# A hybrid decoder layer on one core: sums of the gate and up weights moved from VectorE to accumulating transfers

## The chip, the core and the metric

The kernel runs on one core of one Trainium2 chip. Four of its engines matter here: TensorE (PE, with its weight loads PEld), VectorE (DVE), ScalarE (ACT) and GpSimd (POOL). SyncE (SP) computes nothing and issues the loads from memory. The metric is the time of one execution on the device in microseconds (us); lower is better.

## The reference

A sequence of 16 meta tokens and 512 tokens of width 1024 goes through a half-step SwiGLU feed-forward block, a token mixer (RG-LRU and a convolution, merged by gates), and a second SwiGLU block. Only the two feed-forward blocks are touched:

```python
def swiglu_ffn(h, w_gu, w_down):
    gate, up = jnp.split(h @ w_gu, 2, axis=-1)
    return (jax.nn.silu(gate) * up) @ w_down

h = h + 0.5 * swiglu_ffn(rmsnorm(h, ffn1_norm[l]), ffn1_w_gu[l], ffn1_w_down[l])
h = h + token_mixer(rmsnorm(h, mix_norm[l]), ...)
h = h + 0.5 * swiglu_ffn(rmsnorm(h, ffn2_norm[l]), ffn2_w_gu[l], ffn2_w_down[l])
```

`w_gu` has 1024 rows and 2 x 2816 columns, all in float32.

## The kernel before

**Products.** A float32 product is made from two float32r parts of each operand: a high part (`hi`, a copy by ScalarE) and a low part (`lo`, value minus high part, by VectorE in the feed-forward blocks), in three passes of TensorE.

**Duo groups.** Gate and up are worked off in groups of 256 columns each. The first three groups of each block are plain products. The other eight of each block, 16 in all, go through `duo`: gate and up, each cut into an upper and a lower half of the 1024 rows, form a 2 x 2 block matrix, the tokens' two halves form the other operand, and the result is made with 7 block products in place of 8 (Winograd's form of Strassen's scheme). Each block product has 24 matmuls and takes one "chunk" of weights, 128 partitions x 1024 float32 (512 KB). The seven chunks of a group are four raw blocks or sums of them. In the first feed-forward block the duo groups stand in runs of 1, 4 and 3, with the down projection behind each run; in the second block all eight follow each other.

**Weights.** The class `Weights` holds the whole list of groups. `load` issues a group's loads on SP into the pool `rawp` (7 tiles); `_split` makes the `hi` and `lo` tiles of one chunk (pool `partp`, 5 tiles of each); `take` hands a chunk to the products and keeps three chunks split ahead. Before a chunk that is a sum, `_sums` has VectorE add or subtract raw tiles: per duo group four such operations of 128 x 1024 (`sum1`, `sum2` twice, `sum4`), into the raw tiles themselves and one tile of the pool `sump`.

**Order.** Each engine works off its own queue strictly in order. The order is set when the program is built, by a scheduler that places instructions as soon as it believes their operands ready; it follows the code's order closely inside a duo group. What a duo group puts on ScalarE besides the `hi` copies are the copies of partial results out of PSUM (`g1`, `u2`, `g2` from `al` and `ga`), two Silus, and the `hi` copies of the results (`ah`). The copy of `al` into `g1` must be done before the group's third product, which adds to the same `al`.

Of the kernel before, what the change touches and what calls it, by code (L numbers as in the profile page):

```python
# [9 lines left out]
F32 = mybir.dt.float32  # L10
F32R = mybir.dt.float32r
AF = mybir.ActivationFunctionType
ALU = mybir.AluOpType

P = 128
# [6 lines left out]
DFF = 2816  # L22
# [4 lines left out]
RG_C = 8.0  # L27
UNIT = 544
NUNITS = 61
NRAW = 7  # L30
SUMS_AHEAD = 1
PLAIN1 = 6
PLAIN2 = 6
AHEAD = 3
# [6 lines left out]
CH = 1024  # L41


class Weights:
# [2 lines left out]

    def __init__(self, nc, raw_pool, part_pool, groups, ahead):  # L50
        self.nc, self.raw_pool, self.part_pool = nc, raw_pool, part_pool
        self.groups = groups
        self.chunks = [(g, c) for g, grp in enumerate(groups) for c in range(len(grp["chunks"]))]
        self.ahead = ahead
        self.pin = None
        self.raw = {}
        self.made = {}
        self.next_group = 0
        self.next_chunk = 0
        self.next_sum = 0  # L60
        self.taken = 0

    @staticmethod
# [11 lines left out]
    def load(self, between=None):  # L75
        g = self.next_group
        pieces = []
        i = 0
        for q, (shape, srcs) in enumerate(self.groups[g]["loads"]):
            view = self.shaped(self.raw_pool.tile([P, CH], F32, tag="wraw", name=f"wraw{g}_{q}"), shape)  # L80
            for at, src in srcs:
                self.nc.sync.dma_start(out=view[at] if at is not None else view, in_=src)
                if between is not None:
                    between(i)
                i += 1
            pieces.append(view)
        self.raw[g] = pieces
        self.next_group += 1

# [1 line left out]
        while self.next_group <= min(g, len(self.groups) - 1):  # L91
            self.load()

    def _sums(self, upto):

        while self.next_sum < min(upto, len(self.chunks)):
            g, c = self.chunks[self.next_sum]
            pre = self.groups[g].get("sums", {}).get(c)
            if pre is not None:
                self._loaded(g)  # L100
                pre(self.raw[g])
            self.next_sum += 1

    def _split(self):
        i = self.next_chunk
        g, c = self.chunks[i]
        self._loaded(g + 1)
        self._sums(i + 1)
        grp = self.groups[g]
        src = grp["chunks"][c](self.raw[g])  # L110
        shape = list(src.shape)
        out = []
        for part in ("hi", "lo"):
            flat = self.part_pool.tile([P, CH], F32R, tag="w" + part, name=f"w{part}{i}")
            out.append(self.shaped(flat, shape))
        hi, lo = out
        ins = self.nc.scalar.activation(hi, src, AF.Copy)  # L117
        if self.pin is not None:
            self.pin(ins)
        eng = self.nc.gpsimd if grp["lo"] == "pool" else self.nc.vector  # L120
        ins = eng.tensor_tensor(lo, src, hi.bitcast(F32), op=ALU.subtract)  # L121
        if self.pin is not None and grp["lo"] != "pool":
            self.pin(ins)
        self.made[i] = (hi, lo)
        self.next_chunk += 1
        if self.pin is None:
            self._sums(i + 1 + SUMS_AHEAD)

    def fill(self):
        while self.next_chunk < min(self.taken + self.ahead, len(self.chunks)):  # L130
            self._split()

    def take(self):
        i = self.taken
        while self.next_chunk < min(i + 1 + self.ahead, len(self.chunks)):
            self._split()
        self.taken += 1
        return self.made.pop(i)


# [1 line left out]
def layer_kernel(ctx, tc, a, out):  # L142
# [1 line left out]
    cpool = ctx.enter_context(tc.tile_pool(name="cpool", bufs=1))  # L144
    upool = ctx.enter_context(tc.tile_pool(name="upool", bufs=NUNITS))
    rawp = ctx.enter_context(tc.tile_pool(name="rawp", bufs=NRAW))
    sump = ctx.enter_context(tc.tile_pool(name="sump", bufs=1))
    partp = ctx.enter_context(tc.tile_pool(name="partp", bufs=5))
    psum = ctx.enter_context(tc.tile_pool(name="psum", bufs=3, space=bass.MemoryType.PSUM))
    psum1 = ctx.enter_context(tc.tile_pool(name="psum1", bufs=2, space=bass.MemoryType.PSUM))  # L150
# [57 lines left out]
    def kview(w, k0, nk, c0, ncol):  # L208
        return w[k0 * P:(k0 + nk) * P, c0:c0 + ncol].rearrange("(k p) m -> p k m", p=P)
# [6 lines left out]
    def duo_group(w, f):  # L216


        hk = KT // 2
        loads = [((P, hk, 2 * P), [(None, kview(w, k0, hk, c0, 2 * P))])  # L220
                 for c0, k0 in ((f * P, 0), (DFF + f * P, 0), (DFF + f * P, hk), (f * P, hk))]
        held = {}

        def sum1(raws):
            g1, u1, u2, g2 = raws
            s1 = Weights.shaped(sump.tile([P, CH], F32, tag="wsum", name=f"wsum{count[0]}"), (P, hk, 2 * P))
            count[0] += 1
            held["s1"] = s1
            nc.vector.tensor_tensor(s1, u1, u2, op=ALU.add)

        def sum2(raws):
            g1, u1, u2, g2 = raws
            nc.vector.tensor_tensor(u1, g1, u1, op=ALU.subtract)
            nc.vector.tensor_tensor(g1, held["s1"], g1, op=ALU.subtract)

        def sum4(raws):
            g1, u1, u2, g2 = raws
            nc.vector.tensor_tensor(g2, g2, g1, op=ALU.subtract)

        chunks = [lambda r: r[0], lambda r: held["s1"], lambda r: r[0], lambda r: r[3], lambda r: r[1],  # L240
                  lambda r: r[3], lambda r: r[2]]
        groups.append(dict(loads=loads, chunks=chunks, lo="dve", sums={1: sum1, 2: sum2, 5: sum4}))

    thirds = [(0, 8), (8, 16), (16, 22)]
    for f0, f1 in thirds:
# [286 lines left out]
    def operands(ops, src, norm, r, th):  # L532

        hk = KT // 2
        b = {}

        def quarter(kh):
            for i in range(hk // 2):
                for t in range(2):
                    b[kh, t, i] = pair("xq", th)  # L540
                for j in range(2):
                    k = kh * hk + 2 * i + j
                    for t in range(2):
                        cut = slice(t * th, (t + 1) * th)
                        nc.vector.scalar_tensor_tensor(b[kh, t, i][:, j, :], src[k][:, cut], norm(k), r[:, cut],
                                                       op0=ALU.mult, op1=ALU.mult)

        def minus(eng, x, y, out=None):

            o = [out[i] if out is not None else pair("xt", th) for i in range(2)]  # L550
            for i in range(2):
                eng.tensor_tensor(o[i], x[i], y[i], op=ALU.subtract)
            return o

        def parts(x):
            out = []
            for i in range(2):
                hi, lo = pair("bh", th, F32R), pair("bl", th, F32R)
                nc.scalar.activation(hi, x[i], AF.Copy)
                nc.vector.tensor_tensor(lo, x[i], hi.bitcast(F32), op=ALU.subtract)  # L560
                out += [(hi[:, j, :], lo[:, j, :]) for j in range(2)]
            return out

        def q(kh, t):
            return [b[kh, t, i] for i in range(2)]
        quarter(0)
        yield
        ops[1] = parts(q(0, 0))
        t1 = minus(nc.vector, q(0, 1), q(0, 0))
        yield  # L570
        ops[5] = parts(t1)
        yield
        quarter(1)
        yield
        t2 = minus(nc.vector, q(1, 1), t1)
        ops[6] = parts(t2)
        yield
        t3 = minus(nc.vector, q(1, 1), q(0, 1), q(0, 1))
        ops[2] = parts(q(1, 0))
        yield  # L580
        t4 = minus(nc.vector, q(1, 0), t2, q(1, 0))
        ops[7] = parts(t3)
        yield
        ops[3] = parts(q(1, 1))
        ops[4] = parts(t4)

    def duo(ops, th, scale=None):

        def times(p, ps, first, last):
            whi, wlo = weights.take()  # L590
            for j in range(2):
                cols = slice(j * P, (j + 1) * P)
                for k in range(KT // 2):
                    xhi, xlo = ops[p][k]
                    for n, (w, xx) in enumerate(((whi, xhi), (whi, xlo), (wlo, xhi))):
                        nc.tensor.matmul(ps[:, j, :th], w[:, k, cols], xx,  # L596
                                         start=(first and k == 0 and n == 0),
                                         stop=(last and k == KT // 2 - 1 and n == 2), skip_group_check=True)
# [17 lines left out]
        times(3, ga, False, True)  # L616
        nc.vector.tensor_tensor(g2, ga[:, :, :th], g2, op=ALU.add)
        nc.scalar.activation(g2, g2, AF.Silu)
        if scale is None:
            nc.vector.tensor_tensor(g2, u2, g2, op=ALU.mult)  # L620
        else:
            nc.vector.scalar_tensor_tensor(g2, u2, scale, g2, op0=ALU.mult, op1=ALU.mult)
        times(4, al, False, True)
        if scale is None:
            nc.vector.tensor_tensor(g1, al[:, :, :th], g1, op=ALU.mult)
        else:
            nc.vector.scalar_tensor_tensor(g1, al[:, :, :th], scale, g1, op0=ALU.mult, op1=ALU.mult)
        return g1, g2

    def split_pairs(pairs, th):  # L630
# [448 lines left out]
```

## Time and profile before

| | |
|---|---|
| median of 3 runs | 1195.04 us (1194.33 to 1195.42) |
| the profiled execution | 1196.02 us, of which the span from first to last instruction is 1194.2 us |
| TensorE busy | 1168.1 us, 98% of the span |
| VectorE busy | 828.7 us, 69% |
| ScalarE busy | 536.6 us, 45% |
| GpSimd busy | 263.4 us, 22%, none of it in the duo groups |
| moved by DMA | 115.24 MB |

The profile is of one execution. Busy time of an engine is the time in which one of its instructions ran; idle time matters only on the engine that sets the end, and there the profile names what ended each wait.

### The profile page before, as it was taken

What the parts mean: (1) busy time and instruction counts of PE and PEld (TensorE: products, weight loads), DVE (VectorE), ACT (ScalarE), POOL (GpSimd) and SP (SyncE); (2) the same over time, 40 slices, a digit from 0 to 9 for tenths busy, and PEclk for the clock granted to TensorE, in tenths of its full rate; (3) what the DMA queues carried; (4) which work ended last, traced back from release to release, by engine and by line L of the source; (5) the groups of instructions that cost most, each with busy time, mean ns of one, the idle gap of its engine ahead of it and who ended that gap; (6) DMA issues with size and microseconds to landing.
All of it is one profiled execution on the core that took longest, in us unless ns stands there. A gap on an engine that the chain in (4) does not pass through costs nothing.

```text
span 1194.2 us, 18531 instructions
## 1 busy us (share of the span) xinstructions
PE 1168.1 (98%) x7723; PEld 1072.6 (90%) x7723; DVE 828.7 (69%) x1051; ACT 536.6 (45%) x703; POOL 263.4 (22%) x144
## 2 busy tenths in 40 slices
PE   7999999999999999999989999999999999999997
PEld 6999999999999999998878887878779999998886
DVE  7987468744866799978986907555697787882223
ACT  5544146522545523356666417433444555572113
POOL 5000000000007455565545843442000000000000
PEclk9999999999999999999989999999999999999999
DMA  8515124422253233332223323333212424253201
GB/s 231 159 33 156 50 72 135 130 89 64 65 151 110 84 95 89 94 101 64 78 88 100 95 88 89 90 96 96 89 54 71 142 72 142 71 177 100 76 1 70
DMA packets 165226, 115.24 MB, mean 96 GB/s; under 512 B 3927, under 2 KB 161015, under 8 KB 165143
## 3 DMA queue, kind: packets, MB, share of 16 engines
q1 hardware_dynamic: 163936, 112.74, 31.5%
q8 instruction: 60, 0.98, 0.3%
q10 hardware_dynamic: 1207, 1.33, 0.3%
q14 instruction: 23, 0.19, 0.0%
HBM read 111.95 MB, written 2.10 MB: 96 GB/s over the span
## 4 chain that ended last, share of the span: by engine, by line
PE 89%; DVE 5%; ACT 3%; DMA 1%; issue 1%; SPq 0%; DVEq 0%; ACTq 0%
PE al L596 15%; PE fin L975 10%; PE down L305 10%; PE ga L596 8%; PE g L305 6%; PE gluv L305 4%; PE glug L305 4%; PE be L596 4%; PE ya L305 4%; PE yb L305 4%; PE wo L305 3%; PE up L305 3%; PE gy L305 3%; PE sgb L305 3%; PE gate L305 3%; PE sga L305 2%
## 5 line engine op out<-in xcount | busy, mean ns | idle before, releaser
L117 ACT ACTIVATE whi<-wraw 128x1024 fp32r<-128x1024 f32 (+2 forms) x244 | 254.5, 1045 | 519.5 <-issue 134.8
L121 DVE TENSOR_TENSOR wlo<-wraw,whi 128x1024 fp32r<-128x1024 f32 (+1 forms) x164 | 198.5, 1212 | 140.6 <-ACT whi L117 136.2
L121 POOL TENSOR_TENSOR wlo<-wraw,whi 128x1024 fp32r<-128x1024 f32 (+1 forms) x80 | 204.8, 2564 | 204.9 <-ACT whi L117 204.8
L713 DVE SCALAR_TENSOR_TENSOR conv<-v,par,conv 128x512 f32<-128x512 f32 x240 | 159.2, 747 | 0.0
L596 PE MATMUL al<-bh,whi 128*128 128x264 f32 (+1 forms) x512 | 144.9, 283 | 0.0
L596 PE MATMUL al<-bl,whi 128*128 128x264 f32 (+1 forms) x512 | 144.9, 283 | 0.0
L596 PE MATMUL al<-bh,wlo 128*128 128x264 f32 (+1 forms) x512 | 144.6, 282 | 0.0
L347 POOL TENSOR_TENSOR sq<-sq,sq 128x528 f32<-128x528 f32 (+1 forms) x18 | 28.1, 1559 | 354.0 <-ACT sq L344 353.9
L596 PEld LDWEIGHTS al<-bh,whi 128*128 128x128 f32 x512 | 96.5, 189 | 0.1
L596 PEld LDWEIGHTS al<-bh,wlo 128*128 128x128 f32 x512 | 96.6, 189 | 0.0
L596 PEld LDWEIGHTS al<-bl,whi 128*128 128x128 f32 x512 | 96.4, 188 | 0.0
L305 PE MATMUL down<-al,whi 128*128 128x264 f32 x352 | 72.3, 286 | 2.1 <-DVE al L636 2.1
L596 PE MATMUL ga<-bh,wlo 128*128 128x264 f32 (+1 forms) x256 | 72.5, 283 | 0.0
L596 PE MATMUL ga<-bl,whi 128*128 128x264 f32 (+1 forms) x256 | 72.4, 283 | 0.0
L596 PE MATMUL ga<-bh,whi 128*128 128x264 f32 (+1 forms) x256 | 72.2, 282 | 0.0
L305 PE MATMUL down<-ah,wlo 128*128 128x264 f32 x352 | 71.5, 284 | 0.0
L305 PE MATMUL down<-ah,whi 128*128 128x264 f32 x352 | 71.4, 284 | 0.0
L305 PEld LDWEIGHTS down<-al,whi 128*128 128x128 f32 x352 | 54.9, 188 | 2.6 <-DVE al L636 2.5
L305 PEld LDWEIGHTS down<-ah,wlo 128*128 128x128 f32 x352 | 54.7, 189 | 0.0
L305 PEld LDWEIGHTS down<-ah,whi 128*128 128x128 f32 x352 | 54.5, 188 | 0.0
L684 DVE SCALAR_TENSOR_TENSOR h<-down,h 128x528 f32<-128x528 f32 x24 | 17.0, 708 | 52.4 <-PE down L305 52.4
L596 PEld LDWEIGHTS ga<-bh,whi 128*128 128x128 f32 x256 | 48.3, 189 | 0.0
(278 smaller groups left out, 2937.1 us busy)
## 6 DMA issues: line engine op xcount, KB each, us to landing
wraw<-in_ffn_w_gu_dram SPq DMA_DIRECT2D x86, 512.0 KB
wraw<-in_w_in_dram SPq DMA_DIRECT2D x48, 512.0 KB
wraw<-in_ffn_w_down_dram SPq DMA_DIRECT2D x38, 512.0 KB
wraw<-in_rnn_w_proj_dram SPq DMA_DIRECT2D x8, 512.0 KB
wraw<-in_conv_w_proj_dram SPq DMA_DIRECT2D x8, 512.0 KB
wraw<-in_w_out_dram SPq DMA_DIRECT2D x8, 512.0 KB
wraw<-in_ffn_w_down_dram SPq DMA_DIRECT2D x8, 384.0 KB
x<-in_x_dram SPq DMA_DIRECT2D x8, 256.0 KB
```

Of the source, the lines that this page charges most:

```text
L117: ins = self.nc.scalar.activation(hi, src, AF.Copy)
L121: ins = eng.tensor_tensor(lo, src, hi.bitcast(F32), op=ALU.subtract)
L305: pin(nc.tensor.matmul(o, w, xx[:, tok] if isinstance(tok, slice) else xx[tok], start=(first and n == 0), stop=(last and n == 2)))
L347: (eng or nc.gpsimd).tensor_tensor(acc, acc, sq, op=ALU.add)
L596: nc.tensor.matmul(ps[:, j, :th], w[:, k, cols], xx, start=(first and k == 0 and n == 0), stop=(last and k == KT // 2 - 1 and n == 2), ski ...
L684: nc.vector.scalar_tensor_tensor(halves(h[m]), ps[:, :, :TH], 0.5, halves(h[m]), op0=ALU.mult, op1=ALU.add)
L713: pin(nc.vector.scalar_tensor_tensor(box[i], v[i][:, k:k + SEQ], pcol("conv_dw_w", k * KT + j + i), box[i], op0=ALU.mult, op1=ALU.add))
L975: nc.tensor.matmul(accs[t][c][:, cols], aa[t // 2][:, t % 2 * P:(t % 2 + 1) * P], w[:, c * SEQ + cols.start:c * SEQ + cols.stop], start=Fa ...
```

## The change

The four sums of each duo group are no longer made by VectorE. A raw tile is loaded, and a transfer issued by GpSimd then reads a second block from memory and adds it onto that tile (`accum_op=ALU.add`). Tile 0 is loaded with a21 (up, upper rows), a22 is added at once (chunk 0); after chunk 0 has been split a11 is added (chunk 2), and after chunk 2 a12 (chunk 5). Tile 1 is loaded with a11 (chunk 1), and after chunk 1 a21 is added (chunk 4). a12 and a22 are also loaded as they are (chunks 3 and 6). So a group has four loads as before and four more transfers of 512 KB. [...] The first product takes chunk 1 and the second chunk 0 (`take(1)`). The raw pool has 8 tiles in place of 7, and the pool `sump` is gone.

```diff
-NRAW = 7
-SUMS_AHEAD = 1
+NRAW = 8
...
             pieces.append(view)
+        for piece, src in self.groups[g].get("adds", {}).get(-1, ()):
+            self.nc.gpsimd.dma_start(out=pieces[piece], in_=src, accum_op=ALU.add)
         self.raw[g] = pieces
...
         self.made[i] = (hi, lo)
         self.next_chunk += 1
-        if self.pin is None:
-            self._sums(i + 1 + SUMS_AHEAD)
+        for piece, src in grp.get("adds", {}).get(c, ()):
+            self.nc.gpsimd.dma_start(out=self.raw[g][piece], in_=src, accum_op=ALU.add)
...
-        loads = [((P, hk, 2 * P), [(None, kview(w, k0, hk, c0, 2 * P))])
-                 for c0, k0 in ((f * P, 0), (DFF + f * P, 0), (DFF + f * P, hk), (f * P, hk))]
-        held = {}
-
-        def sum1(raws):
-            g1, u1, u2, g2 = raws
-            s1 = Weights.shaped(sump.tile([P, CH], F32, tag="wsum", name=f"wsum{count[0]}"), (P, hk, 2 * P))
-            count[0] += 1
-            held["s1"] = s1
-            nc.vector.tensor_tensor(s1, u1, u2, op=ALU.add)
-
-        def sum2(raws):
-            g1, u1, u2, g2 = raws
-            nc.vector.tensor_tensor(u1, g1, u1, op=ALU.subtract)
-            nc.vector.tensor_tensor(g1, held["s1"], g1, op=ALU.subtract)
-
-        def sum4(raws):
-            g1, u1, u2, g2 = raws
-            nc.vector.tensor_tensor(g2, g2, g1, op=ALU.subtract)
-
-        chunks = [lambda r: r[0], lambda r: held["s1"], lambda r: r[0], lambda r: r[3], lambda r: r[1],
-                  lambda r: r[3], lambda r: r[2]]
-        groups.append(dict(loads=loads, chunks=chunks, lo="dve", sums={1: sum1, 2: sum2, 5: sum4}))
+        a11, a21, a22, a12 = [kview(w, k0, hk, c0, 2 * P)
+                              for c0, k0 in ((f * P, 0), (DFF + f * P, 0), (DFF + f * P, hk), (f * P, hk))]
+        loads = [((P, hk, 2 * P), [(None, src)]) for src in (a21, a11, a12, a22)]
+
+        chunks = [lambda r, q=q: r[q] for q in (0, 1, 0, 2, 1, 0, 3)]
+        groups.append(dict(loads=loads, chunks=chunks, lo="dve",
+                           adds={-1: [(0, a22)], 0: [(0, a11)], 1: [(1, a21)], 2: [(0, a12)]}))
...
-            whi, wlo = weights.take()
+            whi, wlo = weights.take(1 if p == 1 else 0)
```

VectorE before, at the turn from one duo group (tiles numbered 1643 to 1649) to the next (1940 to 1946). `L121` makes the `lo` part of a chunk; `L229`, `L233`, `L234` and `L238` are the sums:

```order
L121 TENSOR_TENSOR wlo_1949<-wraw_0_1643,whi_1948 128x1024
L234 TENSOR_TENSOR wraw_0_1643<-wsum_1952,wraw_0_1643 128x1024
L612 TENSOR_TENSOR g_156_1845<-be_1909,g_156_1845 128x528
L121 TENSOR_TENSOR wlo_1980<-wsum_1952,whi_1979 128x1024
L229 TENSOR_TENSOR wsum_2185<-wraw_1_1942,wraw_2_1944 128x1024
L615 TENSOR_TENSOR u_158_1877<-al_1816,u_158_1877 128x528
L121 TENSOR_TENSOR wlo_2013<-wraw_0_1643,whi_2012 128x1024
L233 TENSOR_TENSOR wraw_1_1942<-wraw_0_1940,wraw_1_1942 128x1024
L617 TENSOR_TENSOR g_159_1907<-ga_1847,g_159_1907 128x528
L121 TENSOR_TENSOR wlo_2051<-wraw_3_1649,whi_2050 128x1024
L620 TENSOR_TENSOR g_159_1907<-u_158_1877,g_159_1907 128x528
L238 TENSOR_TENSOR wraw_3_1649<-wraw_3_1649,wraw_0_1643 128x1024
```

In the change these four are gone from VectorE, which keeps the `lo` parts and the PSUM work in the same order.

GpSimd's queue in the change, over the same run of groups (now numbered 1640, 1936, 2168). `L88` is the first add onto a tile 0 (a22, behind the load), `L118` are the adds behind a split, in the order a11 onto tile 0, a21 onto tile 1, a12 onto tile 0:

```order
L88 DMA wraw_0_1936<-in_ffn_w_gu_dram 128x4x256
L118 DMA wraw_0_1640<-in_ffn_w_gu_dram 128x4x256
L118 DMA wraw_1_1642<-in_ffn_w_gu_dram 128x4x256
L118 DMA wraw_0_1640<-in_ffn_w_gu_dram 128x4x256
L88 DMA wraw_0_2168<-in_ffn_w_gu_dram 128x4x256
L118 DMA wraw_0_1936<-in_ffn_w_gu_dram 128x4x256
L118 DMA wraw_1_1938<-in_ffn_w_gu_dram 128x4x256
L118 DMA wraw_0_1936<-in_ffn_w_gu_dram 128x4x256
```

Before, GpSimd had nothing to do between the first plain group and the last down projection of this block. Now each group's first add stands ahead of the three later adds of the group before it.

ScalarE's queue in the change, from chunk 2 of group 1640 on. `L108` makes `hi` of a chunk, `L589`, `L593` and `L596` copy PSUM results:

```order
L108 ACTIVATE whi_2007<-wraw_0_1640 128x1024
L108 ACTIVATE whi_2046<-wraw_2_1644 128x1024
L605 ACTIVATE g_157_1903<-g_157_1903 128x528
L108 ACTIVATE whi_2103<-wraw_1_1642 128x1024
L616 ACTIVATE ah_2037<-g_154_1842 128x528
L616 ACTIVATE ah_2041<-g_157_1903 128x528
L108 ACTIVATE whi_2107<-wraw_0_1640 128x1024
L589 ACTIVATE g_164_2074<-al_2045 128x528
L108 ACTIVATE whi_2138<-wraw_3_1646 128x1024
L593 ACTIVATE u_166_2101<-ga_2076 128x528
```

The order is nearly that of before (one `ah` has moved ahead of the `hi` copy of chunk 5). What is new is what these wait for: `whi_2007` (chunk 2) now waits for the add of a11, and `whi_2107` (chunk 5) for the add of a12, with the copy of `al` right behind it.

## Rows read from the trace of the kernel before

**Rows 1.** The page, busy time of the engines over the span.
```profile
PE 1168.1 (98%) x7723; PEld 1072.6 (90%) x7723; DVE 828.7 (69%) x1051; ACT 536.6 (45%) x703; POOL 263.4 (22%) x144
```

**Rows 2.** What TensorE waited for: total us, times, longest us.
```profile
PE rg L305 <- DVE xrl L334: 6.4, 3, 2.4
...
PE down L305 <- DVE al L636: 2.1, 2, 1.9
...
PE g L305 <- ACT whi L117: 0.9, 1, 0.9
```

**Rows 3.** The chain that ended last: start us, length us, what.
```profile
173.94 5.86 PE al L596 x48
179.80 2.91 PE ga L596 x24
182.71 2.92 PE al L596 x24
...
245.66 42.38 PE down L305 x345
```

**Rows 4.** The same chain, two pieces of it that are loads.
```profile
108.45 3.59 DMA wraw<-in_ffn_w_gu_dram
...
238.38 5.29 DMA wraw<-in_ffn_w_gu_dram
```

**Rows 5.** Instructions on a tile: duration ns min/median/max, first and last start.
```profile
L121 POOL TENSOR_TENSOR wlo<-wraw,whi x80: 1262/2404/5996, 6.5 to 806.9; 128x1024 fp32r<-128x1024 f32 x76, 128x512 fp32r<-128x512 f32 x4
...
L229 DVE TENSOR_TENSOR wsum<-wraw,wraw x16: 1218/1224/1226, 46.5 to 1017.0; 128x1024 f32<-128x1024 f32 x16
...
L238 DVE TENSOR_TENSOR wraw<-wraw,wraw x16: 1212/1218/1227, 85.7 to 1042.9; 128x1024 f32<-128x1024 f32 x16
```

**Rows 6.** VectorE by line, 156.4 to 238.4: count | busy, mean ns.
```profile
L620 DVE TENSOR_TENSOR g<-u,g 128x528 f32<-128x528 f32 x4 | 2.8, 700 | 0.0
...
L684 DVE SCALAR_TENSOR_TENSOR h<-down,h 128x528 f32<-128x528 f32 x1 | 0.7, 709 | 2.5 <-PE down L305 2.5
```

**Rows 7.** VectorE's instructions in order: start us, length us, what [idle before].
```profile
166.22 1.23 DVE L121 TENSOR_TENSOR wlo<-wraw,whi 128x1024 fp32r<-128x1024 f32 x1 [1.69 <-ACT whi L117]
...
172.25 1.21 DVE L121 TENSOR_TENSOR wlo<-wraw,whi 128x1024 fp32r<-128x1024 f32 x1
```

**Rows 8.** ScalarE's instructions in order, the same stretch.
```profile
170.98 1.06 ACT L117 ACTIVATE whi<-wraw 128x1024 fp32r<-128x1024 f32 x1 [0.98 <-PE al L596]
...
179.77 1.06 ACT L117 ACTIVATE whi<-wraw 128x1024 fp32r<-128x1024 f32 x1 [0.37 <-PE al L596]
180.74 0.63 ACT L635 ACTIVATE ah<-g 128x528 fp32r<-128x528 f32 x1
181.27 0.59 ACT L602 ACTIVATE g<-al 128x528 f32<-128x528 f32 x1
```

**Rows 9.** Stretches: us, PE, PEld, DVE, ACT, POOL busy, PEclk, DMA share, GB/s.
```profile
156.40:176.90 20.50, 20.50 (x171) 20.50 (x170) 15.00 (x16) 10.13 (x13) 0.00 (x0) 1.00 0.29 89
...
992.00:1012.00 20.00, 20.00 (x172) 20.00 (x171) 15.94 (x16) 10.27 (x13) 0.00 (x0) 1.00 0.35 109
```

**Rows 10.** DMA queues: packets, MB, share of 16 engines.
```profile
q1 hardware_dynamic: 163936, 112.74, 31.5%
```

**Rows 11.** SP's issue of the loads: duration ns min/median/max.
```profile
L82 SPq DMA_DIRECT2D wraw<-in_ffn_w_gu_dram x90: 367/368/2597, 1.7 to 1025.2; - x90
```

**Rows 12.** The same columns, around two waits of TensorE in the mixer.
```profile
548.00:551.00 3.00, 1.08 (x9) 0.87 (x7) 3.00 (x3) 2.31 (x2) 3.00 (x2) 1.00 0.61 175
551.00:554.00 3.00, 2.94 (x17) 2.91 (x18) 3.00 (x6) 0.77 (x2) 2.25 (x1) 0.75 0.55 180
554.00:557.00 3.00, 3.00 (x10) 2.32 (x9) 3.00 (x6) 0.64 (x1) 1.31 (x1) 0.69 0.61 175
580.00:583.00 3.00, 1.64 (x11) 1.29 (x9) 3.00 (x2) 2.34 (x2) 3.00 (x2) 1.00 0.59 174
583.00:586.00 3.00, 2.40 (x18) 2.36 (x19) 3.00 (x5) 0.85 (x2) 2.80 (x1) 1.00 0.60 171
```

More of the change, by code (lines that the diff above doesn't have):

```diff
@@ L57, in __init__ @@
         self.made = {}
+        self.early = set()
         self.next_group = 0
         self.next_chunk = 0
-        self.next_sum = 0
         self.taken = 0
@@ L92, in _loaded @@
             self.load()
[L94 to L102, printed above, removed]
     def _split(self):
@@ L107, in _split @@
         self._loaded(g + 1)
-        self._sums(i + 1)
         grp = self.groups[g]
@@ L131, in fill, with take @@
             self._split()
-    def take(self):
-        i = self.taken
-        while self.next_chunk < min(i + 1 + self.ahead, len(self.chunks)):
+    def take(self, place=0):
+        i = self.taken + place
+        while self.next_chunk < i + 1:
             self._split()
-        self.taken += 1
+        while self.next_chunk < min(self.taken + 1 + self.ahead, len(self.chunks)):
+            self._split()
+        if place == 0:
+            self.taken += 1
+            while self.taken in self.early:
+                self.early.remove(self.taken)
+                self.taken += 1
+        else:
+            self.early.add(i)
         return self.made.pop(i)
@@ L146, in layer_kernel @@
     rawp = ctx.enter_context(tc.tile_pool(name="rawp", bufs=NRAW))
-    sump = ctx.enter_context(tc.tile_pool(name="sump", bufs=1))
     partp = ctx.enter_context(tc.tile_pool(name="partp", bufs=5))
@@ L546, in quarter, with minus @@
                                                        op0=ALU.mult, op1=ALU.mult)
-        def minus(eng, x, y, out=None):
+        def minus(x, y, out=None, neg=False):
             o = [out[i] if out is not None else pair("xt", th) for i in range(2)]
             for i in range(2):
-                eng.tensor_tensor(o[i], x[i], y[i], op=ALU.subtract)
+                if neg:
+                    nc.vector.scalar_tensor_tensor(o[i], x[i], -1.0, y[i], op0=ALU.mult, op1=ALU.subtract)
+                else:
+                    nc.vector.tensor_tensor(o[i], x[i], y[i], op=ALU.subtract)
             return o
@@ L568, in operands @@
         ops[1] = parts(q(0, 0))
-        t1 = minus(nc.vector, q(0, 1), q(0, 0))
+        t1 = minus(q(0, 0), q(0, 1))
         yield
@@ L574, in operands @@
         yield
-        t2 = minus(nc.vector, q(1, 1), t1)
+        t2 = minus(t1, q(1, 1), neg=True)
         ops[6] = parts(t2)
         yield
-        t3 = minus(nc.vector, q(1, 1), q(0, 1), q(0, 1))
+        t3 = minus(q(1, 1), q(0, 1), q(0, 1))
         ops[2] = parts(q(1, 0))
         yield
-        t4 = minus(nc.vector, q(1, 0), t2, q(1, 0))
+        t4 = minus(t2, q(1, 0), q(1, 0), neg=True)
         ops[7] = parts(t3)
@@ L585, in operands, with duo @@
         ops[4] = parts(t4)
-    def duo(ops, th, scale=None):
+    def duo(ops, th, scale=1.0):
         def times(p, ps, first, last):
-            whi, wlo = weights.take()
+            whi, wlo = weights.take(1 if p == 1 else 0)
             for j in range(2):
@@ L618, in duo @@
         nc.scalar.activation(g2, g2, AF.Silu)
[L619 to L622, printed above, removed]
+        nc.vector.scalar_tensor_tensor(g2, u2, -scale, g2, op0=ALU.mult, op1=ALU.mult)
         times(4, al, False, True)
[L624 to L627, printed above, removed]
+        nc.vector.scalar_tensor_tensor(g1, al[:, :, :th], -scale, g1, op0=ALU.mult, op1=ALU.mult)
         return g1, g2
```

## The prediction

> **What bounds the kernel now.** I read the page's list of engines first. TensorE is busy for 1168.1 of 1194.2 us [rows 1], so whatever is taken from another engine is worth only what TensorE waits for that engine. The list of TensorE's waits comes next: on VectorE's part it waits 2.1 us for `al` of a duo group, at two places, and 6.4 us for `xrl` in the mixer, where no weight sums are made; 0.9 us go to a weight split [rows 2]. Third, the chain that ended last: inside a duo group the block products follow each other without a gap, 2.92 us for each 24 matmuls (20.4 us for a group of seven), where a down projection takes 42.38 us for 345 matmuls, 5.9 us for 48, one chunk [rows 3]. The stretches say the same: 20.50 of 20.50 us busy, at full clock, with VectorE at 15.0 [rows 9]. So VectorE is not what the duo groups wait for, and the sums that are taken away lie beside TensorE's work.
>
> **What is removed.** 64 operations of 1.22 us on VectorE (four kinds, 16 of each, two of them shown) [rows 5], 78 us off the path. What can come back of it is the wait for `al`, where the first sum of the next run stands ahead of the last `al` and waits for a late load: 2.1 us at most. The two multiplications per group that become three-operand ones cost the same: 0.700 us against 0.709 [rows 6]. [...]
>
> **What is added.** 64 transfers of 512 KB with an add, which now stand on a chain of their own: low part of chunk 0, add of a11, split of chunk 2, add of a12, high part of chunk 5. ScalarE works strictly in order, and behind the high part of chunk 5 stands the copy of `al`, for which the group's third product waits. So the question is whether two adds fit into this chain's time.
>
> *The time there is.* In the trace of before, VectorE ends the low part of chunk 0 at 166.22 + 1.23 = 167.45 [rows 7]. ScalarE starts the high part of chunk 5 at 179.77, which takes 0.97 until the next instruction, and the copy of `al` takes 0.59 [rows 8]; the third product of the next group begins at 182.71 [rows 3]. So the high part may start as late as 182.71 - 1.56 = 181.15. Between lie 13.7 us. The split of chunk 2, from 170.98 [rows 8] to 172.25 + 1.21 = 173.46 [rows 7], needs 2.5 of them. **11.2 us are left for two adds.** In the first group of a run (1, 4, 3 and 8 groups) the early splits are paced by products of 5.9 us [rows 3], so there two adds fit; the other 12 groups pay what is above 11.2 us, each one anew, because the next group's splits are released by TensorE's progress.
>
> *What an add takes.* No row shows one. The nearest is a load of the same size: 3.59 and 5.29 us from the release to the data, where it stands on the chain [rows 4]. The loads' queue moved 112.74 MB in 31.5% of 1194.2 us [rows 10], 300 GB/s, so 512 KB are 1.75 us of all engines and 1.84 us of the 3.59 are fixed. The transfer of an add is at least that 1.75 and, if the destination must be read besides the source, 3.5. The issue is at least SP's 0.37 [rows 11]; GpSimd's own row for a tile of this size is 2.40 [rows 5]. I take 3.5, since an add has two inputs, and an issue of 1.2, between the ends. One add is then 1.84 + 1.2 + 3.5 = 6.5, two are 13.1. They do not have the DMA engines to themselves: on GpSimd's queue the first add of the next group stands ahead of the add of a11, and SP's loads are released at the same time; one such transfer beside the two is 1.75 (a load) to 3.5 (an add); I take 2.6. **15.7 against 11.2: 4.5 us for each of 12 groups, 54 us.**
>
> Two pages of the Trainium skill speak to this, against each other. "DMA: Bandwidth & Descriptors", section "Anatomy of one DMA", fits a transfer issued by GpSimd as 2.0 us plus bytes over 436 GB/s; by that estimate an add would be 3.2 us, two 6.4, and nothing would be lost; the 3.59 us of the load agree with the fit, but neither it nor any row here is of a transfer that adds. "Collectives: The Full Stack", section "The bandwidth ceiling: the fold count and why AG ≠ RS ≠ AR", says that an add in the DMA engines needs two source reads and goes at half the rate of a copy; by that the transfer is the upper of my two ends, and the sum stands. No run here shows it.
>
> *The clock.* After the wait of 1.9 us at 548 to 551 the granted clock fell to 0.75 and 0.69 for 6 us, in which 0.75 + 0.93 = 1.7 us were lost; after one of 2.0 us at 580 to 586 it stayed at 1.00 [rows 12]. A wait of 4.5 us per group is longer than both, so I add 1.7 us in each of the 12 groups: 20 us.
>
> *The sum.* 1196.0 (the profiled execution) + 54 + 20 - 2 = 1268. That execution lies 1.0 us above the median of the runs, so I forecast **1267 us**. With the neighbour at 1.75 to 3.5 us and the clock falling never or always it is 1237 to 1279.
>
> **The rivals.**
> - *The adds are hidden.* With the low ends (1.84 + 0.37 + 1.75 = 4.0, two 7.9, and a load of 1.75 beside them 9.7) they fit into 11.2. What speaks for it: the DMA engines are only 0.29 to 0.35 busy in the duo groups [rows 9]. The time is then that of before, less up to 2.1 us: 1193 to 1195. The point at which it turns is an add of 5.6 us with everything in it.
> - *A little over.* With 2.6 for the transfer and 1.0 for the issue, 2 x 5.4 + 1.75 = 12.6: 1.4 us over, 12 times, and waits too short for the clock: 17 us, 1210.
> - *The queue or the DMA engines become the bound.* With 2.4 us of issue for each add and both neighbours in the way, 2 x (1.84 + 2.4 + 3.5) + 3.5 + 1.75 = 20.7, 9.5 over, 114 us, with the clock 1327. The same comes out if an add keeps the engines three times as long as a load: 4 x 1.75 + 4 x 5.25 = 28 us of them in a group of 20.4, 7.6 over in 16 groups, 122 us. For it: four adds at 3.5 and four loads already make 21.0, just above a group's time.
> - *Faster.* If the 2.1 us of `al` and the 0.9 us for a weight split [rows 2] both go, since VectorE is free and an eighth raw tile lets loads start earlier, and no add is late: 1195.0 - 3.0 = 1192. It needs adds of under 5.6 us and both places at once.
>
> **How the numbers follow.** 0.2% of this kernel, 2.4 us, is about what its measurement can tell from no change. The forecast (above 1225 and up to 1300) 0.47, a little over 0.13, far over 0.17, hidden 0.20, faster 0.03. So faster 0.03, same 0.20, slower 0.77. The range 1193 to 1315 holds the hidden case, the little and the forecast one, and leaves out the faster one and most of the far one, together 0.17 or so.
>
> **What would show each step.** In the profile after: the 64 sums gone from VectorE, which falls by about 78 us; 64 GpSimd transfers and 33.6 MB more moved, and a new queue whose share of the engines per MB is twice that of q1 if the destination's read counts. Waits of ScalarE's `whi` for a DMA, several us each, two per group, and of TensorE's `al` products for ScalarE; no such waits in the first group of a run; the group's length at 25 us in place of 20.4; clock below 1.00 in the duo groups only. The prediction is wrong if an add lands within 5.6 us of the end of its split (then nothing changes), or if the groups lengthen by far more than 4.5 us, which would show as DMA share near 1.0 or a GpSimd queue that is never empty.

## The result, and the profile after

The kernel with the adding transfers takes 1239.61 us (median of 4 runs, 1235.03 to 1240.34) against 1195.23 us before on the same chip: ratio 1.0354, interval 1.033 to 1.0379, so 44 us more. The forecast was 1267 us, in a range of 1193 to 1315. The profiled execution has a span of 1237.8 us, 43.6 more than before [rows 1].

The page after: busy time of the engines, the two DMA queues that carry weights (packets, MB, share of 16 engines), GpSimd's issues (count | busy, mean ns | idle before) and the transfers with their median us from issue to landing.

```profile
PE 1184.5 (96%) x7723; PEld 1087.7 (88%) x7723; DVE 758.3 (61%) x987; ACT 532.1 (43%) x703; POOL 345.9 (28%) x208
...
q1 hardware_dynamic: 163936, 112.74, 30.3%
q0 software_dynamic: 33792, 33.56, 18.3%
...
L118 POOL DMA_DIRECT2D wraw<-in_ffn_w_gu_dram x48 | 61.6, 1283 | 292.3 <-DVE wlo L112 270.5
...
wraw<-in_ffn_w_gu_dram POOLq DMA_DIRECT2D x64, 512.0 KB, 6.1
```

VectorE is relieved of 70 us (forecast: 78). In this kernel up also enters with its sign turned (`neg=True` in `minus`, `-scale` in the two last multiplications); that work is part of VectorE's 758.3 us. TensorE is busy for 16.4 us more than before with the same 7723 matmuls: its clock was lower, 0.980 on average in place of 0.994. The new queue q0 holds 18.3% of the 16 engines for 33.56 MB, 0.545% for each MB, where q1 needs 0.269%: an add keeps the DMA engines twice as long as a load. 18.3% of 1237.8 us over 64 adds is 3.54 us for each.

What TensorE waited for (total us, times, longest us):

```profile
PE al L583 <- ACT g L589: 27.2, 11, 3.8
PE rg L288 <- DVE xrl L317: 6.4, 3, 2.4
```

The wait for `al` on VectorE [rows 2] is gone; 11 waits for ScalarE's copy of `al` (L589) have come, none of them in the first group of a run. 27.2 us of waits and 16.4 us of slower matmuls are 43.6, as much as the span has grown; the 2.1 us of [rows 2] that went came back in small waits elsewhere.

One group in the middle of the run of eight, on GpSimd and ScalarE in order of time (start us, length us, what, [idle before and what ended it]):

```profile
946.28 1.28 POOL L88 DMA_DIRECT2D wraw<-in_ffn_w_gu_dram  x1 [6.67 <-DMA wraw<-in_ffn_w_gu_dram]
953.11 1.28 POOL L118 DMA_DIRECT2D wraw<-in_ffn_w_gu_dram  x1 [5.54 <-DVE wlo L112]
955.90 1.28 POOL L118 DMA_DIRECT2D wraw<-in_ffn_w_gu_dram  x1 [1.52 <-DVE wlo L112]
961.87 1.28 POOL L118 DMA_DIRECT2D wraw<-in_ffn_w_gu_dram  x1 [4.68 <-DVE wlo L112]
...
959.26 2.01 ACT L108 ACTIVATE whi<-wraw 128x1024 fp32r<-128x1024 f32 x2 [4.39 <-DMA wraw<-in_ffn_w_gu_dram]
...
967.99 1.06 ACT L108 ACTIVATE whi<-wraw 128x1024 fp32r<-128x1024 f32 x1 [4.20 <-DMA wraw<-in_ffn_w_gu_dram]
968.95 0.58 ACT L589 ACTIVATE g<-al 128x512 f32<-128x512 f32 x1
...
969.58 0.39 PE L583 MATMUL al<-bh,whi 128*128 128x256 f32 x1 [2.02 <-ACT g L589]
```

Read it as the chain of the prediction. GpSimd's rows are the first add of the next group (946.28), then a11, a21 and a12. The add of a11 starts at 953.11, and chunk 2's high part at 959.26: 6.15 us. 2.61 us later the add of a12 starts, and chunk 5's high part at 967.99: 6.12 us. Behind it stands the copy of `al`, and TensorE has waited 2.02 us for that. Over the whole execution, an add takes this long from issue to landing (us, min/median/max; first the 48 adds behind a split, L118, then the 16 first adds, L88):

```profile
DMA to landing us min/median/max: 5.7/6.1/8.0
DMA to landing us min/median/max: 5.8/7.7/8.9
```

So the 6.1 of the page is the price of the adds on the chain, and the first adds are dearer; no run isolates why.

The clock in stretches around this wait and around the next one of 1.58 us that ends at 992.87 (us, PE, PEld, DVE, ACT, POOL busy, PEclk, DMA share, GB/s), and two products of 24 matmuls from the chain that ended last, the first right behind the last wait, the second later in the same group. PEclk is the granted clock as a share of full speed. The DMA share counts a packet's whole time where the packet starts, so a short stretch can come out above 1:

```profile
966.00:969.00 3.00, 1.56 (x14) 1.35 (x12) 0.00 (x0) 1.01 (x2) 0.00 (x0) 1.00 1.15 313
969.00:972.00 3.00, 2.42 (x15) 2.42 (x16) 2.45 (x2) 1.96 (x4) 0.80 (x1) 0.79 0.51 143
972.00:975.00 3.00, 3.00 (x19) 3.00 (x18) 0.00 (x0) 0.93 (x1) 0.48 (x1) 0.64 0.78 230
975.00:978.00 3.00, 3.00 (x28) 3.00 (x27) 1.92 (x2) 1.62 (x4) 1.28 (x1) 1.00 1.18 229
990.00:993.00 3.00, 1.42 (x12) 1.22 (x12) 0.63 (x1) 1.72 (x3) 0.00 (x0) 1.00 1.11 343
993.00:996.00 3.00, 3.00 (x26) 3.00 (x27) 1.82 (x2) 1.30 (x3) 1.28 (x1) 1.00 0.51 105
```

```profile
1090.41 4.52 PE al L583 x24
...
1103.46 2.85 PE al L583 x24
```

After the wait of 2.02 us the granted clock is 0.79 and 0.64 for two stretches (partly at the lower level, 1.2 GHz, partly at 2.4); after the one of 1.58 us it stays at 1.00. Behind the last and longest wait, 3.79 us, a product of 24 matmuls takes 4.52 us where its like takes 2.85. The group is now 24.1 us long in the run of eight: the third product starts at 945.90 in the second group and at 1090.41 six groups later. The 20.4 us of [rows 3] are of the first block, whose products have 264 columns; in the run of eight they have 256, and before, third product to third product, a group took 949.17 - 929.29 = 19.9 us there (rows of before; the middle one is VectorE's low part of chunk 0, which is needed further below):

```profile
929.29 2.85 PE al L596 x24
...
933.21 1.23 DVE L121 TENSOR_TENSOR wlo<-wraw,whi 128x1024 fp32r<-128x1024 f32 x1 [1.63 <-ACT whi L117]
...
949.17 2.85 PE al L596 x24
```

### The profile page after: what moved, and what is told of

It is laid out like the page before. It is cut to its first block, busy times and chain, and to the rows that moved or that the text cites. A ratio compares the mean times of both kernels' runs of the same rounds, so it can differ in the third digit from the quotient of the medians.

```text
span 1237.8 us, 18624 instructions
## 1 busy us (share of the span) xinstructions
PE 1184.5 (96%) x7723; PEld 1087.7 (88%) x7723; DVE 758.3 (61%) x987; ACT 532.1 (43%) x703; POOL 345.9 (28%) x208
## 3 DMA queue, kind: packets, MB, share of 16 engines
q0 software_dynamic: 33792, 33.56, 18.3%
## 5 line engine op out<-in xcount | busy, mean ns | idle before, releaser
L108 ACT ACTIVATE whi<-wraw 128x1024 fp32r<-128x1024 f32 (+2 forms) x260 | 269.8, 1044 | 590.4 <-issue 127.0
L112 DVE TENSOR_TENSOR wlo<-wraw,whi 128x1024 fp32r<-128x1024 f32 (+1 forms) x180 | 217.9, 1211 | 221.9 <-ACT whi L108 216.4
L583 PE MATMUL al<-bh,whi 128*128 128x264 f32 (+1 forms) x512 | 153.1, 299 | 27.2 <-ACT g L589 27.2
L583 PE MATMUL al<-bl,whi 128*128 128x264 f32 (+1 forms) x512 | 151.5, 296 | 0.0
L583 PE MATMUL al<-bh,wlo 128*128 128x264 f32 (+1 forms) x512 | 151.1, 295 | 0.0
L118 POOL DMA_DIRECT2D wraw<-in_ffn_w_gu_dram x48 | 61.6, 1283 | 292.3 <-DVE wlo L112 270.5
L583 PEld LDWEIGHTS al<-bh,whi 128*128 128x128 f32 x512 | 103.3, 202 | 29.6 <-ACT g L589 29.5
L583 PEld LDWEIGHTS al<-bl,whi 128*128 128x128 f32 x512 | 103.5, 202 | 0.1
L583 PEld LDWEIGHTS al<-bh,wlo 128*128 128x128 f32 x512 | 103.5, 202 | 0.0
L88 POOL DMA_DIRECT2D wraw<-in_ffn_w_gu_dram x16 | 20.7, 1293 | 179.3 <-DMA wraw<-in_ffn_w_gu_dram 106.0
```

Source lines behind the costliest of these rows:

```text
L88: self.nc.gpsimd.dma_start(out=pieces[piece], in_=src, accum_op=ALU.add)
L118: self.nc.gpsimd.dma_start(out=self.raw[g][piece], in_=src, accum_op=ALU.add)
L583: nc.tensor.matmul(ps[:, j, :th], w[:, k, cols], xx, start=(first and k == 0 and n == 0), stop=(last and k == KT // 2 - 1 and n == 2), ski ...
```

## The experiments

Two theories were to be told apart. **The chain**: two adds in series overrun the time between the low part of chunk 0 and the copy of `al`. **The traffic**: 33.6 MB more, at double cost, crowd the DMA engines or hold the tiles, wherever the adds stand. Each ratio is to the kernel before on the same chip, with its 95% interval.

### Off the chain: e1_adds_unread, e2_one_add_less, e3_plain_copy

In the first, all 64 adds are issued, the one of a12 behind chunk 3 in place of chunk 2, but chunks 2 and 5 are read from tiles as loaded (the product sums are others):

```diff
-        chunks = [lambda r, q=q: r[q] for q in (0, 1, 0, 2, 1, 0, 3)]
+        chunks = [lambda r, q=q: r[q] for q in (0, 1, 3, 2, 1, 2, 3)]
...
-  adds={-1: [(0, a22)], 0: [(0, a11)], 1: [(1, a21)], 2: [(0, a12)]}))
+  adds={-1: [(0, a22)], 0: [(0, a11)], 1: [(1, a21)], 3: [(0, a12)]}))
```

In the second the add of a12 is left out; in the third the 64 transfers copy in place of adding:

```diff
-  adds={-1: [(0, a22)], 0: [(0, a11)], 1: [(1, a21)], 2: [(0, a12)]}))
+  adds={-1: [(0, a22)], 0: [(0, a11)], 1: [(1, a21)]}))
...
-  self.nc.gpsimd.dma_start(out=self.raw[g][piece], in_=src, accum_op=ALU.add)
+  self.nc.gpsimd.dma_start(out=self.raw[g][piece], in_=src)
```

> All 64 adds are issued as in the changed kernel, same sizes, same queue and almost the same order, but nothing waits for the two on tile 0 behind chunk 0: chunk 2 is read from tile 3 and chunk 5 from tile 2, as loaded (so these two sums are left out of the result, and the add of a12 is issued behind chunk 3). Chain theory (two adds of some 6 us do not fit between the split of chunk 0 and the latest start of chunk 5): no wait of the al products, 1193 to 1198 us. Traffic theory (33.6 MB more, and the loads that they slow, cost the time): still near 1239 us, and the loads show as the cause of waits.

> The add of a12 on tile 0 is left out, so chunk 5 is split from what chunk 2 was (that sum is left out of the result); 48 adds remain. Chain theory: one add of 6 to 7 us with 11.2 us of room, no waits, 1193 to 1198 us, and the granted clock back at 0.994. Traffic theory: a quarter of the added traffic goes and a quarter of the loss, about 1228 us.

> GpSimd issues the same 64 transfers on the same tiles with the same waits, but as plain copies (the tile is overwritten; the sums are left out of the result). Chain theory with the destination's read as the dear part: a transfer takes 1.75 us of the engines in place of 3.54, lands some 1.8 us earlier, two take about 9 us against 11.2: 1193 to 1200 us, the software queue's share near 9%. If the issue by GpSimd and the fixed part are the dear part, the landing stays near 6 us and the time near 1235 us.

Measured: 1200.72 us, ratio 1.0045 (1.0028 to 1.0061), for the first; 1194.59, 0.9996 (0.9985 to 1.0008), for the second; 1192.56, 0.9974 (0.9964 to 0.9985), for the third. The first lies 2.7 us above the chain's range, the other two in it or 0.4 us below it. So 39 of the 44 us go when nothing reads two adds in series, though every byte is still moved. In the first, 5.8 us of waits for the copy of `al` stay, 5 in number. The longest, 2.6 us, stands in the run of one, where ScalarE had been idle for 5.1 us among parameter loads that it issues itself, and no add ended it. The other four, 3.1 us, are of the kind seen above: chunk 4 still reads the add of a21, which in that kernel is issued within 3.2 us behind two others. GpSimd's and ScalarE's rows there:

```profile
976.14 1.28 POOL L88 DMA_DIRECT2D wraw<-in_ffn_w_gu_dram  x1 [10.47 <-DMA wraw<-in_ffn_w_gu_dram]
976.89 1.84 POOL L118 DMA_DIRECT2D wraw<-in_ffn_w_gu_dram  x1
979.29 1.28 POOL L118 DMA_DIRECT2D wraw<-in_ffn_w_gu_dram  x1 [0.56 <-DVE wlo L112]
...
988.62 2.01 ACT L108 ACTIVATE whi<-wraw 128x1024 fp32r<-128x1024 f32 x2 [4.62 <-DMA wraw<-in_ffn_w_gu_dram]
```

From its issue at 979.29 to the read at 988.62 are 9.3 us, against 6.1 for an add on the chain of the change. The three adds land 6.5, 9.0 and 9.2 us after their issues, at about 982.6, 985.9 and 988.5: one behind the other, some 3 us apart, where one transfer keeps the engines for 3.5 us.

The page of the third (q0 and the issues, columns as above) shows what the adding itself costs:

```profile
q0 software_dynamic: 9216, 33.56, 8.9%
...
L118 POOL DMA_DIRECT2D wraw<-in_ffn_w_gu_dram x48 | 36.0, 749 | 286.7 <-DVE wlo L112 265.2
...
wraw<-in_ffn_w_gu_dram POOLq DMA_DIRECT2D x64, 512.0 KB, 4.0
```

The same bytes as copies take half the engines' time (8.9% of 1190.5 us over 64 is 1.66 us), a little over a quarter of the packets, an issue of 0.75 us in place of 1.28, and land after 4.0 us in place of 6.1. Two of 4.0 fit into the chain, and no wait for `al` is left. The 2.75 us below the kernel before are also the most that any run shows the sums off VectorE to be worth. The profiled execution is 3.7 us shorter than the one before, and only 0.6 of that is idle time of TensorE (25.5 us against 26.1); the rest is its busy time, 1165.0 against 1168.1.

### One add more on the chain: e6_third_add

```diff
-  adds={-1: [(0, a22)], 0: [(0, a11)], 1: [(1, a21)], 2: [(0, a12)]}))
+  adds={-1: [(0, a22)], 0: [(0, a11)], 1: [(1, a21)], 2: [(0, a12), (0, a12)]}))
```

> The add of a12 is issued twice in every group, the second waiting for the first (a12 is counted twice, so the sum of chunk 5 is another number). 80 transfers instead of 64. Theory: each group after the first of a run becomes longer by a whole further add of 6.0 to 7.4 us, since the room is already used up; 12 groups make 72 to 89 us more, and with half-clock stretches of 0 to 1.7 us a group 1310 to 1350 us. Rival (traffic in proportion): a quarter more added bytes, 1239 + 11 = about 1250 us.

Measured: 1294.6 us, ratio 1.0829 (1.0814 to 1.0843): 55 us above the kernel with one a12, below the chain's 1310 and far above the traffic's 1250. The reason for the 55 is in ScalarE's rows: the program's scheduler had put the copy of `al` (L589) ahead of chunk 5's high part here.

```profile
965.44 1.04 ACT L108 ACTIVATE whi<-wraw 128x1024 fp32r<-128x1024 f32 x1
966.90 0.60 ACT L589 ACTIVATE g<-al 128x512 f32<-128x512 f32 x1 [0.42 <-PE al L583]
977.50 2.00 ACT L108 ACTIVATE whi<-wraw 128x1024 fp32r<-128x1024 f32 x2 [10.00 <-DMA wraw<-in_ffn_w_gu_dram]
979.41 0.58 ACT L593 ACTIVATE u<-ga 128x512 f32<-128x512 f32 x1
979.88 1.04 ACT L108 ACTIVATE whi<-wraw 128x1024 fp32r<-128x1024 f32 x1
980.83 0.59 ACT L596 ACTIVATE g<-al 128x512 f32<-128x512 f32 x1
```

The next copy of `al` (L596, for g2) waits in its place:

```profile
PE al L583 <- ACT g L596: 63.3, 11, 7.3
```

The kernel to compare with is the next one, which has that order with one a12: 1294.6 - 1218.2 = 76 us. Of the 73 us between the two profiled executions, 16.7 are TensorE's slower clock (busy for 1193.8 us against 1177.1) and 56 are idle time, 4.7 for each of 12 groups. That is less than the 6.5 us that lie between the issues of the two adds of a12 (964.57 and 971.04). This comparison was made after the run, not before it.

### Other orders of the same 64 adds: e4_copy_first, e8_copy_and_first_moved, e9_high_part_last

The first puts chunk 5's high part behind the copy of `al` for g1. The second also puts the first add of the next group behind the add of a12 on GpSimd's queue. The third, without these two, makes the split of chunk 5 only after the copy for g2.

```diff
+        with self.behind.pop(c, nullcontext)():
+            ins = self.nc.scalar.activation(hi, src, AF.Copy)
...
+        copy = nc.scalar.activation(g1, al[:, :, :th], AF.Copy)
+        weights.behind[5] = lambda: tc.issue_after(copy.ins)
```

```diff
+        if c == 2 and "adds" in grp and g + 1 < len(self.groups):
+            with self.after(add):
+                self.first(g + 1, self.raw[g + 1])
```

```diff
+        copy = nc.scalar.activation(g2, al[:, :, :th], AF.Copy)
+        with tc.issue_after(copy.ins):
+            weights._split()
```

> The changed kernel with one thing moved: ScalarE's high part of chunk 5 is queued behind the copy of al into g1, not ahead of it. The adds, the traffic and all waits for data stay. Chain theory: the add of a12 then has until about 5 us later (the copy of the third product's result, before the fifth product) instead of 1.4 us, the 2.5 us of each of the 11 waits fit: waits of al on g1 gone, clock back, 1193 to 1199 us. Traffic theory, or a theory that the adds as such are too slow for a group's length: 1225 us and more.

> As the kernel with the copy of al queued first on ScalarE (1218 us), and in addition the first add of the next group stands on GpSimd's queue behind the add of a12 of the present group instead of ahead of its add of a11; the whole result is computed. If what is left there (23 us over the kernel before) is GpSimd's queue, where an add of a11 that is ready stands behind a first add that still waits for its load, and the transfer beside it: 1195 to 1203 us, with chunk 2's high part 6.0 to 7.2 us after the start of a11's add instead of 8.6. If the serial chain itself is what is left (the operand of chunk 5 is late for TensorE even without the copy behind it): about 1218 us, with the same waits for al and ga. If the first add now comes too late for chunk 0 of the next group: over 1218 us, with a wait for al at a group's start.

> The kernel of the change with all 64 adds and the same serial pair; only the split of chunk 5 is made one step later in the program, so that on ScalarE its high part stands behind the copies of al (g1), ga (u2) and al (g2) of its group and ahead of none of them; the product that reads it starts some 5.7 us behind g2's copy. The whole result is computed. If the 44 us are only what waits in order behind that one high part: 1195 to 1203 us, no wait for al behind a copy, clock 0.99. If the pair of adds is too long for the group whatever stands behind it (the period of a group is set by add, split, add, split), or if the adds' traffic costs it: 1215 to 1240 us.

Measured: 1218.22 us, ratio 1.0191 (1.0174 to 1.0208); 1226.67, 1.0261 (1.0243 to 1.0279); 1224.71, 1.0239 (1.0225 to 1.0254). All are faster than the change, none comes near the kernel before, and the chain theory's figure failed three times. The first lies between its two theories' figures. The second and the third fit what was stated for the cases that a first add comes too late, and that the pair or the traffic costs the time in any order. What TensorE waited for in each, in this order:

```profile
PE al L585 <- ACT g L599: 7.7, 5, 2.9
...
PE ga L585 <- DVE g L607: 5.9, 4, 1.8
```

```profile
PE al L594 <- ACT g L608: 19.9, 9, 4.1
```

```profile
PE al L587 <- ACT g L593: 18.3, 9, 3.4
```

The wait moves and stays. In the first it goes to the copy of `al` for g2 and to VectorE's sum behind the low part (L607). In the second to the copy for g2 behind chunk 0 of the next group, whose first add is now late. In the third back to the copy for g1, this time behind chunk 2. Besides, TensorE waits once in the run of four for VectorE's copy of `par`, which stands in order behind a low part whose high part waits for an add (in the third the low part starts at 202.00 after 6.32 us of idle time, the copies of `par` at 204.37): not at all before, 1.0 us in the change, 2.5, 2.1 and 5.1 us in these three, and 2.8 and 5.0 in the kernels e5_last_sum_by_vector and e10_vector_sum_last below. The row of the third:

```profile
PE pt L462 <- DVE par L463: 5.1, 1, 5.1
```

GpSimd's and ScalarE's rows of the third show how the adds become late:

```profile
969.17 1.28 POOL L88 DMA_DIRECT2D wraw<-in_ffn_w_gu_dram  x1 [7.37 <-issue]
972.64 2.61 POOL L118 DMA_DIRECT2D wraw<-in_ffn_w_gu_dram  x2 [2.18 <-DVE wlo L112]
...
981.94 1.06 ACT L108 ACTIVATE whi<-wraw 128x1024 fp32r<-128x1024 f32 x1 [10.06 <-DMA wraw<-in_ffn_w_gu_dram]
```

A later split of chunk 5 makes those behind it late too, so a11 and a21 are issued together (x2), 3.5 us behind the first add of the next group, and chunk 2 is read 9.3 us after a11's issue. In one group of e4_copy_first the first add starts 3.07 us ahead of a11's (936.43 and 939.50), and chunk 2 is read 8.6 us after it (948.07), in the next four groups 8.0 to 9.5; in e8_copy_and_first_moved the first add stands right behind a12's, and chunk 5 is read 7.0 us after that (983.27 - 976.31).

### Fewer adds: e5_last_sum_by_vector, e10_vector_sum_last, e7_first_add_only

In the first, VectorE makes the last sum of a group and the other three stay transfers; the second has this and the later split of e9_high_part_last. In the third only a22 is added by a transfer, and VectorE makes the other three sums (the list of chunks as in the first).

```diff
-        chunks = [lambda r, q=q: r[q] for q in (0, 1, 0, 2, 1, 0, 3)]
+        chunks = [lambda r, q=q: r[q] for q in (0, 1, 0, 2, 1, 2, 3)]
...
-  adds={-1: [(0, a22)], 0: [(0, a11)], 1: [(1, a21)], 2: [(0, a12)]}))
+  adds={-1: [(0, a22)], 0: [(0, a11)], 1: [(1, a21)]}, last=3))
...
+        if c == grp.get("last"):
+            r = self.raw[g]
+            self.nc.vector.tensor_tensor(r[2], r[2], r[0], op=ALU.add)
```

```diff
+  adds={-1: [(0, a22)]}, sums={1: (0, 0, 1, ALU.add), 2: (1, 0, 3, ALU.subtract), 3: (2, 2, 0, ALU.add)}))
...
+        if c in grp.get("sums", {}):
+            r = self.raw[g]
+            o, x, y, op = grp["sums"][c]
+            self.nc.vector.tensor_tensor(r[o], r[x], r[y], op=op)
```

> a22, a11 and a21 are still added by transfers (48 of 64), but the last sum of a group, the operand of chunk 5, is made by VectorE from tile 2 and tile 0 as soon as chunks 2 and 3 are split; the whole result is computed. The serial chain of a group then holds one add of about 6 to 7 us and a VectorE sum of 1.2 us. Theory (two adds in series overrun a room of 11.2 us): no wait of TensorE for al behind ScalarE's copy, clock 0.99, 1193 to 1196 us. Rival (the adds' traffic and their hold on the tiles): still three quarters of the added transfers, so about three quarters of the 44 us: 1225 to 1230 us.

> The same later split of chunk 5, with its operand summed by VectorE (48 of 64 adds by transfers, as in the kernel that took 1208 us). The whole result is computed. If the 12 us left there were the copies of al behind the high part: 1192.5 to 1196 us, equal to the kernel before or up to 0.2% faster. If they were the traffic of 25 MB or the hold on the tiles: about 1208 us.

> Only a22 is added by a transfer (16 of 64), right after tile 0 is loaded; VectorE makes the other three sums of a group in the tiles in place: r0 += a11 after chunk 1, a11 + a21 as r0 - a22 after chunk 2, r2 += r0 after chunk 3; the whole result is computed. Theory: no transfer stands in the chain of a group; 1192 to 1195.5 us, so equal to the kernel before or up to 0.25% faster by the 2.1 us that TensorE waited for al there. Rival (traffic in proportion): 1195 + 11 = 1206 us.

Measured: 1207.82 us, ratio 1.0103 (1.0089 to 1.0116); 1217.16, 1.0184 (1.0165 to 1.0202); 1194.95, 0.9997 (0.9988 to 1.0006). The third met the theory's figure; the first two missed it, by 12 and 21 us, and lie outside their rivals' figures (1225 to 1230 us, 1208 us) as well. Rows of the first:

```profile
976.38 1.28 POOL L88 DMA_DIRECT2D wraw<-in_ffn_w_gu_dram  x1 [14.02 <-DVE wlo L112]
979.52 1.28 POOL L121 DMA_DIRECT2D wraw<-in_ffn_w_gu_dram  x1 [1.86 <-DVE wlo L112]
...
987.99 2.01 ACT L108 ACTIVATE whi<-wraw 128x1024 fp32r<-128x1024 f32 x2 [6.66 <-DMA wraw<-in_ffn_w_gu_dram]
...
993.89 1.06 ACT L108 ACTIVATE whi<-wraw 128x1024 fp32r<-128x1024 f32 x1 [1.37 <-DVE wraw L119]
```

The add of a11 has the first add of the next group 3.1 us ahead of it and takes 8.5 us. From chunk 2's high part to chunk 5's are 5.9 us more, in which VectorE's sum stands behind its other work. In all 14.4 us, hardly less than the 14.9 of the two adds in the change, and TensorE waits 1.4 us for the copy. In ten such waits 7.5 us were lost; TensorE's busy time in the profiled execution, 1168.7 us, shows no loss to the clock. In e10_vector_sum_last the adds of a11 and a21 are issued together some 4 to 5 us behind the first add, and chunk 2 is read 6.7 and 8.9 us later in two successive groups. So one add is enough to be late if it has company and if what replaces the other costs as much. No version that computes the whole result is faster than the kernel before.

## Why the prediction was right, and where it was off

- **The sums lie off the path: right.** They leave VectorE, and the most that any run shows this to be worth is the 2.75 us of e3_plain_copy (forecast: 2.1 at most, 3.0 for all places together).
- **The chain and the place of the wait: right.** TensorE's `al` waits for ScalarE's copy behind chunk 5's high part; none in the first group of a run, 11 instead of 12 in the others. e1_adds_unread and e2_one_add_less take the serial pair apart, and 39 and 45 us are back. In e1_adds_unread the DMA share is higher than in the change (0.97 against 0.88, see the row below), so it is not the traffic as such.
- **The price of one add: right, in part by luck.** Two of its parts were picked between ends, and both came out: issue 1.28 us (taken 1.2), transfer 3.54 (taken 3.5), in all 6.1 (taken 6.5; the fixed part is 6.15 - 1.28 - 3.54 = 1.3, not 1.84). The page "Collectives: The Full Stack" of the Trainium skill, "The bandwidth ceiling: the fold count and why AG ≠ RS ≠ AR", has the adding step of a ring of cores at half a copy's rate, because the add reads two sources. The queues' shares here, on one core, agree with half the rate: 0.545% against 0.269% for each MB. The fit in the Trainium skill's "DMA: Bandwidth & Descriptors", "Anatomy of one DMA", gives an estimate of 3.2 us for such a transfer; the measured 6.1 for an add and 4.0 for a copy decide against it here. The load's 3.59 us, which the prediction calls in agreement with the fit, are 0.4 above it and of a load that SP issued.
- **The neighbour, the mis-sized term.** I let 2.6 us of another transfer lie beside the two adds, because the first add of the next group stands ahead of a11's on the queue. It does stand there, but starts 5.4 to 8.7 us ahead in the run of eight (946.28 against 953.11), and with its median of 7.7 us it is nearly over. Two adds cost 6.15 + 6.12 = 12.3 us in the group shown, not 15.7. Where an add stands closely ahead, the size of 2.6 is of the right order: 8.5 us in the rows of e5_last_sum_by_vector, 8.0 to 9.5 in e4_copy_first, so 1.9 to 3.4 more than 6.1.
- **The room: 1.0 us too wide.** In the group shown the third product, without its wait, would have begun 969.58 - 2.02 - 953.11 = 14.45 us after a11's start. Less the split between the adds (2.61) and high part and copy (1.6) 10.2 us are left for two adds, against the 11.2 read from before. About half of the difference was there to be read: the forecast took the room from a group of the first block, from the end of chunk 0's low part to the third product 182.71 - 167.45 = 15.26 us, but seven of the 12 paying groups stand in the run of eight. There the same stretch was 949.17 - 933.21 - 1.23 = 14.73 us before (rows in the section on the result). The rest is mainly that an add starts 0.3 us after the low part's end (953.11 after 952.81). 12.3 - 10.2 is about the 2.0 us of wait in this group; the mean over 11 is 2.5, where the forecast had 4.5: 27 us in place of 54.
- **The clock: right in kind, 16.4 us in place of 20.** It fell after nine of the eleven waits (2.0 to 3.8 us) and stayed at 1.00 after those of 1.18 and 1.58 us. The length of the wait alone does not decide it, see the last section.
- **The sum and the range.** Of the 72 us that were forecast 44 came: the neighbour and the price made the sum too large, the room made it too small. The range of 1193 to 1315 held the hidden case as well, so that the time lies in it says little for the mechanism; the waits and the first three experiments do.
- **The rivals.** "Hidden" was the case to fear, and e3_plain_copy shows it with transfers of 4.0 us, below the turning point of 5.6. "The DMA engines become the bound" did not come true at the forecast size, but it was nearer than the 1327 us suggest: the row below is the run of eight in e1_adds_unread, with a DMA share of 0.97 and TensorE still busy for 126.9 of 130 us.

```profile
930.00:1060.00 130.00, 126.88 (x1064) 126.05 (x1064) 74.59 (x78) 63.30 (x81) 29.64 (x23) 1.00 0.97 209
```

Over the same stretch the DMA share is 0.88 in the change, where TensorE is busy for 119.2 us, and 0.66 in e3_plain_copy. What stays open: whether the orders of e4_copy_first, e8_copy_and_first_moved and e9_high_part_last are slow by the serial pair alone or by adds that meet on the queue and the engines (share 0.88 and 0.87 in the first and the third); no run separates the two, since each order changed both. More raw tiles, which would let the first adds start earlier, were not tried.

## What to carry to other kernels

Work that is moved from an engine with time to spare to a transfer becomes a latency: count how many such transfers stand one behind the other between two uses of the same buffer, and what waits in order behind the last reader. In this kernel an add by transfer of 512 KB is 6 us where the add ahead of it on the queue is nearly done, and 8 to 10.8 us where one or two are still under way (10.8 is the longest at L118 in e1_adds_unread). So one of them needs the time of two to four products of 2.85 us, and two in series need more than this kernel's group has. If the engine that is relieved is off the path, the change can win little more than the few waits for it, which is worth reading off the profile before anything is moved.

## What the runs showed of the hardware beyond that

- The adding, not the queue, makes the transfer dear: from the same queue 33.56 MB took 9216 packets, 0.75 us of issue and 1.66 us of the engines for each transfer as copies, 33792 packets, 1.28 us and 3.54 us as adds.
- TensorE's ten waits of up to 1.42 us in e5_last_sum_by_vector, and the one of 1.58 us in the change, cost nothing of the clock; the one of 2.02 us was followed by 0.79 and 0.64, the one of 3.79 us by a product of 4.52 us in place of 2.85. But a wait of 3.30 us in e9_high_part_last left the clock at 1.00 (the rows are the first matmul after it and the next 3 us), and one of 1.75 us in e8_copy_and_first_moved was followed by 0.57. What decides is open.

```profile
1033.39 0.39 PE L587 MATMUL al<-bh,whi 128*128 128x256 f32 x1 [3.30 <-ACT g L593]
...
1033.00:1036.00 3.00, 2.61 (x22) 2.61 (x23) 1.96 (x2) 0.83 (x2) 0.08 (x1) 1.00 0.77 104
```
